# Hybrid decoder layer, input projection: all four chunks of a unit as seven half-size products, with two weight sums added by the load

## The chip, the cores and the metric

One core of a Trainium2 chip runs the whole layer. The metric is the device time of one execution in microseconds (us); the median of three runs of the kernel before is 972.0 us (971.56 to 974.65).

## What is computed

x (512 tokens by 2048, float32) is multiplied by one wide matrix; its columns feed 16 heads of 128 in three kinds (6 forgetting, 6 stick-breaking, 4 differential), each with query, key, value and gate. Each head's causal attention is multiplied by SiLU of its gate, the heads are joined, go through an output projection, and end in a layer norm:

```python
h = x @ w_in
(fq, fk, fv, fg, sq, sk, sv, sg, dq, dk, dv, dg, ff) = jnp.split(h, _split_points(), axis=-1)
...
o_fox = o_fox.reshape(b, s, FOX_W) * jax.nn.silu(fg)
...
y = jnp.concatenate([o_fox, o_sb, o_d], axis=-1) @ w_out
return _layernorm(DEEPNORM_ALPHA * x + y, ln_g, ln_b)
```

## The kernel before

Every float32 operand of a large product is cut into a high and a low part: ACT casts the high one, DVE subtracts it for the low one (`split`, L123, with `low`, L120). A product is then three matmuls, high by high, high by low and low by high (`mm3`, L111).

**Units and chunks.** Heads go in 8 pairs. A unit is one of a pair's four projections (query, key, value, gate): 256 columns of the weights by all 512 tokens, over 2048 inputs. Its weights come in four chunks of 512 inputs, 512 KB each, j = 0 to 3. The first two units are done together in eight chunks of another layout ("f"); 30 units of four chunks follow, u = 2 to 31, and then the output projection ("o"). `load_chunk` (L153) issues a chunk's load on SP's queue and its cuts on ACT and DVE, two chunks ahead of PE (`AHEAD`); raw chunks have three buffers, each cut part two.

**Seven products.** Chunks j = 1, 2, 3 (`SJ`) are taken as two-by-two blocks, with seven products of half the size in place of eight (Winograd's form of Strassen's method). `seven` (L188) makes four sums of weight blocks into the tile t (L193 two at once, L195, L196), and cuts the blocks in three tiles: a (products 1 and 2), t (5, 7, 6, 4) and d (3). The sums of the tokens' blocks are made once, by POOL, in `x_sums` (L306), out of raw tiles that `load_x` (L293) fetches while the first eight chunks run. A product is 2 k-tiles by three matmuls of 256 columns, 42 matmuls a chunk, in the order of `SEVEN`; `BANK` says which half of which PSUM bank (a to d) each goes to.

**The plain chunk.** Chunk j = 0 (`CJ`) comes last in a unit, as ordinary products straight into banks c and d: 24 products of 512 columns, of which one is taken as two halves. While it runs, ACT and DVE empty banks a and b into the tile e (L759 to L763); after it, DVE adds e to banks c and d (L786) to give the unit's two heads.

**Order of the work.** Matmuls stay in program order. `tick` (L218) counts 16 steps a unit, and `at_unit` (L215) hangs other work on a step: attention of the pairs (`attend`), and the moving of results. The other engines' order comes from the framework's planner. The second head's query and key wait in tiles of their own (`qk_tile`, L432) until `evac_later` (L436) cuts them.

## Time and profile before

| | |
|---|---|
| median of three runs | 972.0 us |
| the profiled execution | 972.67 us |
| its span, first to last instruction | 970.9 us |
| PE, DVE, ACT, POOL busy | 98%, 78%, 53%, 15% |
| bytes moved | 108.74 MB, 112 GB/s in the mean |
| granted TensorE clock, mean | 0.993 |

The span is the time between the first and the last instruction; the execution's own time adds 1.8 us. Busy shares are means over stages with different limits, so the stages are read one by one. Matmuls overlap: the time that one costs is read from one start to the next, not from its duration.

### The profile page before, as it was taken

How to read it: one execution, taken by the hardware profiler on the slowest of the kernel's cores; microseconds unless marked ns; L12 is line 12 of the kernel's file. 1: busy time of each engine (PE TensorE's matmuls, PEld its weight loads, DVE VectorE, ACT ScalarE, POOL GpSimd, SP SyncE). 2: the span in 40 equal slices, each digit the busy share in tenths (PEclk: the TensorE clock that was granted, in tenths of full speed). 3: DMA queues.
4: the chain of work that ended last, by engine and by line, in shares of the span. 5: the costliest groups of instructions: out<-in, count | busy, mean ns of one | idle time of the engine just before them, and what ended most of it. 6: DMA issues, size and time to landing. Idle time of an engine off the chain costs nothing.

```text
span 970.9 us, 16701 instructions
## 1 busy us (share of the span) xinstructions
PE 949.8 (98%) x6406; PEld 873.8 (90%) x6406; DVE 759.1 (78%) x1388; ACT 518.7 (53%) x965; POOL 141.9 (15%) x162
## 2 busy tenths in 40 slices
PE   9998999999999999999999999999999999999994
PEld 8988999999999998999899999999999988888883
DVE  7879898988898988999999888778877853442558
ACT  6556655675466556755675657446645852212222
POOL 4320211030103000110010012100201010000026
PEclk9999999999999999999999999999999999999998
DMA  7521233233223322223223333333332634833413
GB/s 282 155 79 58 99 89 122 74 109 108 98 88 98 99 87 87 85 83 105 78 90 107 109 109 99 98 99 98 109 109 98 225 100 120 325 92 104 125 38 140
DMA packets 33559, 108.74 MB, mean 112 GB/s; under 512 B 4034, under 2 KB 4674, under 8 KB 33224
## 3 DMA queue, kind: packets, MB, share of 16 engines
q1 hardware_dynamic: 29256, 95.63, 30.6%
q10 hardware_dynamic: 3744, 10.49, 3.0%
q0 software_dynamic: 480, 1.57, 0.7%
q8 instruction: 50, 0.82, 0.4%
q14 instruction: 29, 0.24, 0.1%
HBM read 99.80 MB, written 7.88 MB: 111 GB/s over the span
## 4 chain that ended last, share of the span: by engine, by line
PE 89%; DVE 5%; issue 3%; DMA 1%; ACT 1%; POOL 0%; ACTq 0%; SPq 0%; DVEq 0%; POOLq 0%
PE o L106 10%; PE l L106 3%; PE pt L109 2%; PE p0a L106 1%; PE p0b L106 1%; PE po0a L106 1%; PE po0b L106 1%; PE po0d L106 1%; PE po0c L106 1%; PE po2d L106 1%; PE po2c L106 1%; PE po2b L106 1%; PE po2a L106 1%; PE p0c L106 1%; PE p0d L106 1%
## 5 line engine op out<-in xcount | busy, mean ns | idle before, releaser
L121 DVE TENSOR_TENSOR wlt<-t,wht 128x1024 fp32r<-128x1024 f32 x90 | 110.7, 1230 | 17.9 <-ACT wht L126 17.8
L121 DVE TENSOR_TENSOR wl<-raw,wh 128x1024 fp32r<-128x1024 f32 x53 | 64.8, 1222 | 59.1 <-ACT wh L126 58.8
L126 ACT CAST wht<-t 128x1024 fp32r<-128x1024 f32 x90 | 94.3, 1048 | 28.7 <-DVE t L196 14.6
L126 ACT CAST wh<-raw 128x1024 fp32r<-128x1024 f32 x53 | 55.6, 1049 | 66.0 <-PE po2d L106 27.6
L126 ACT CAST wha<-raw 128x512 fp32r<-128x512 f32 x90 | 55.6, 619 | 48.6 <-PE p18c L106 3.6
L121 DVE TENSOR_TENSOR wla<-raw,wha 128x512 fp32r<-128x512 f32 x90 | 65.3, 727 | 15.0 <-ACT wha L126 14.7
L193 DVE TENSOR_TENSOR t<-raw 128x512 f32<-128x512 f32 x90 | 64.9, 721 | 0.5
L510 ACT ACTIVATE u<-u,m 128x128 f32<-128x128 f32 (+3 forms) x56 | 31.5, 562 | 48.8 <-DVE m L507 48.6
L121 DVE TENSOR_TENSOR wld<-raw,whd 128x256 fp32r<-128x256 f32 x90 | 50.1, 556 | 0.3
L126 ACT CAST pth<-pt 128x128 fp32r<-128x128 f32 (+1 forms) x64 | 27.0, 422 | 22.9 <-PE pt L109 22.8
L196 DVE TENSOR_TENSOR t<-raw,t 128x256 f32<-128x256 f32 x90 | 37.9, 421 | 1.5
L457 POOL TENSOR_TENSOR g<-g,ge 128x512 f32<-128x512 f32 x16 | 26.9, 1680 | 82.7 <-ACT ge L456 82.7
L195 DVE TENSOR_TENSOR t<-raw,t 128x256 f32<-128x256 f32 x90 | 38.0, 423 | 0.9
L126 ACT CAST whd<-raw 128x256 fp32r<-128x256 f32 x90 | 36.0, 400 | 4.5 <-PE p21d L106 1.6
L523 POOL TENSOR_SCALAR_AFFINE_SELECT d<-d 128x128 f32<-128x128 f32 x24 | 14.8, 618 | 158.9 <-ACT d L522 138.0
L468 POOL TENSOR_TENSOR mx<-mx,g 128x512 f32<-128x512 f32 x14 | 20.2, 1445 | 119.7 <-issue 101.1
L121 DVE TENSOR_TENSOR ptl<-pt,pth 128x128 fp32r<-128x128 f32 (+1 forms) x64 | 31.0, 484 | 5.3 <-ACT pth L126 5.0
L879 POOL TENSOR_TENSOR y<-y,gb 128x512 f32<-128x512 f32 (+1 forms) x8 | 12.0, 1517 | 157.9 <-ACT y L878 157.9
L182 DVE TENSOR_TENSOR wl<-raw,wh 128x512 fp32r<-128x512 f32 x22 | 16.0, 746 | 17.8 <-ACT wh L181 17.8
L760 DVE TENSOR_TENSOR e<-e 128x256 f32<-128x256 f32 x30 | 13.7, 456 | 18.5 <-ACT e L759 18.0
L543 POOL TENSOR_SCALAR_AFFINE_SELECT e<-e 128x128 f32<-128x128 f32 x24 | 10.4, 434 | 118.2 <-DVE e L542 90.3
L106 PE MATMUL o<-ptl,vh 128*128 128x256 f32 x96 | 26.9, 280 | 0.0
(6718 smaller groups left out, 3809.1 us busy)
## 6 DMA issues: line engine op xcount, KB each, us to landing
raw<-in_w_in_dram SPq DMA_DIRECT2D x120, 512.0 KB, 3.5
raw<-in_w_out_dram SPq DMA_DIRECT2D x32, 512.0 KB, 3.5
xr<-in_x_t_dram SPq DMA_DIRECT2D x7, 512.0 KB, 4.6
raw<-in_w_first_dram SPq DMA_DIRECT2D x7, 512.0 KB, 5.4
mixd<-mx SPq DMA_DIRECT2D x14, 256.0 KB, 2.0
mr<-mixd ACTq DMA_DIRECT2D x14, 256.0 KB, 4.1
out_dram<-y SPq DMA_DIRECT2D x14, 256.0 KB, 2.3
y<-in_x_dram ACTq DMA_DIRECT2D x4, 768.0 KB, 9.1
```

Of the source, the lines that this page charges most:

```text
L106: pin(T.matmul(ps, lhs, rhs, start=start, stop=stop))
L109: pin(T.transpose(dst, src, idt))
L121: V.tensor_tensor(out=lo, in0=src, in1=hi.bitcast(F32), op=ALU.subtract)
L126: A.copy(hi, src)
L182: pin(V.tensor_tensor(out=lo, in0=raw[:, k], in1=hi.bitcast(F32), op=ALU.subtract))
L193: V.tensor_tensor(out=t[:, 0:2], in0=raw[:, :, P:].rearrange("p (b k) c -> p b k c", b=2), in1=raw[:, 0:2].rearrange("p k (b c) -> p b k c ...
L195: V.tensor_tensor(out=t[:, 2], in0=b22, in1=t[:, 0], op=ALU.subtract)
L196: V.tensor_tensor(out=t[:, 3], in0=b21, in1=t[:, 2], op=ALU.subtract)
L457: G.tensor_tensor(out=c, in0=c, in1=e, op=ALU.mult)
L468: G.tensor_tensor(out=mx, in0=mx, in1=gt[h], op=ALU.mult)
L510: A.activation(u[:, :n], u[:, :n], AF.Exp, bias=m, scale=-1.0, accum_out=sm)
L523: G.affine_select(out=dt_[:, i * P:n], in_=dt_[:, i * P:n], pattern=[[-1, P]], base=0, channel_multiplier=1, compare_op=ALU.is_ge, fill=BIG)
```

## The change

All four chunks of a unit, in the order 0 to 3, are taken as seven products, in the order 1, 6, 5, 7, 2, 4, 3, so that both products of a bank follow each other. In the last chunk `combine` empties each bank as soon as its last product is done. The weight blocks are laid out so that all four sums are additions: SP loads the raw chunk and, apart, block b11; POOL issues a transfer of blocks 1 and 2 that adds them to the landed blocks 0 and 1; DVE makes the other two sums in place, after blocks 2 and 3 have been cut. The tokens' sums change signs to match, are made for all eight raw tiles, and take raw buffers. The tiles t, qc, kc and others go; the second head's query and key pass through a DRAM tensor `qkd`, written and read back by POOL's queue.

```diff
@@ -61,17 +61,14 @@
     return out
-SJ = (1, 2, 3)
-CJ = tuple(j for j in range(NK // 4) if j not in SJ)
 NRES = 3
 AHEAD = 2
 T0 = 32
 TU = 16
 PAIRS = [(ORDER[2 * p], ORDER[2 * p + 1]) for p in range(NK // 2)]
-SEVEN = (1, 5, 7, 6, 2, 4, 3)
+SEVEN = (1, 6, 5, 7, 2, 4, 3)
 BANK = {1: ("a", 0), 6: ("a", 1), 5: ("b", 0), 7: ("b", 1), 2: ("c", 0), 4: ("c", 1), 3: ("d", 0)}
 H2 = S // 2
-XTAGS = ["t", "ptl", "e", "pth", "ptl", "e", "ptl", "e"]
...
@@ -137,7 +134,7 @@
     NJ = NK // KC
     NU = 4 * len(PAIRS)
     chunks = [("f", 0, j) for j in range(NJ)]
-    chunks += [("u", u, j) for u in range(2, NU) for j in SJ + CJ]
+    chunks += [("u", u, j) for u in range(2, NU) for j in range(NK // 4)]
     N_OUT = len(chunks)
     chunks += [("o", g, j) for g in range(4) for j in range(NJ)]
     ready = {}
@@ -154,14 +151,9 @@
         kind, g, j = chunks[n]
         if kind == "u":
-            raw = raw_tile(f"raw{n}", [P, 4, 256])
+            raw = raw_tile(f"raw{n}", [P, 4, 2, P])
             nc.sync.dma_start(raw, w_in[g - 2, j])
-            if j in SJ:
-                ready[n] = seven(n, raw)
-            else:
-                parts = part_tiles(n, [P, 4, 256])
-                split(*parts, raw)
-                ready[n] = [tuple(t[:, k] for t in parts) for k in range(4)]
+            ready[n] = seven(n, raw, w_in[g - 2, j])
             return
         raw = raw_tile(f"raw{n}", [P, KC, 512])
         if kind == "f":
@@ -185,24 +177,23 @@
             split(*parts, raw)
             ready[n] = [tuple(t[:, k] for t in parts) for k in range(KC)]
-    def seven(n, raw):
-
-        b21, b22 = raw[:, 2:4, :P], raw[:, 2:4, P:]
-        t = wpool.tile([P, 4, 2, P], F32, tag="t", bufs=1, name=f"t{n}")
-
-        V.tensor_tensor(out=t[:, 0:2], in0=raw[:, :, P:].rearrange("p (b k) c -> p b k c", b=2),
-                        in1=raw[:, 0:2].rearrange("p k (b c) -> p b k c", b=2), op=ALU.subtract)
-        V.tensor_tensor(out=t[:, 2], in0=b22, in1=t[:, 0], op=ALU.subtract)
-        V.tensor_tensor(out=t[:, 3], in0=b21, in1=t[:, 2], op=ALU.subtract)
-        fa = part_tiles(f"a{n}", [P, 4, P], "t2")
-        split(*fa, raw[:, :, :P])
+    def seven(n, raw, src):
+
+
+        b11 = wpool.tile([P, 2, P], F32, tag="b11", bufs=2, name=f"b11_{n}")
+        nc.sync.dma_start(b11, src[:, 0])
+        nc.gpsimd.dma_start(raw[:, 0:2], src[:, 1:3], accum_op=ALU.add)
+        f1 = part_tiles(f"a{n}", [P, 2, P], "t1")
+        split(*f1, b11)
+        f2 = part_tiles(f"b{n}", [P, 2, 2, P], "t2")
+        split(*f2, raw[:, 2:4])
+
+        V.tensor_tensor(out=raw[:, 2], in0=raw[:, 2], in1=raw[:, 0], op=ALU.add)
+        V.tensor_tensor(out=raw[:, 3], in0=raw[:, 3], in1=raw[:, 2], op=ALU.add)
         ft = part_tiles(f"t{n}", [P, 4, 2, P])
-        split(*ft, t)
-        fd = part_tiles(f"d{n}", [P, 2, P], "t1")
-        split(*fd, b22)
-        return {1: [f[:, 0:2] for f in fa], 2: [f[:, 2:4] for f in fa], 3: fd,
-                5: [f[:, 0] for f in ft], 7: [f[:, 1] for f in ft],
-                6: [f[:, 2] for f in ft], 4: [f[:, 3] for f in ft]}
+        split(*ft, raw)
+        factor = {1: (f1, None), 3: (f2, 0), 2: (f2, 1), 5: (ft, 0), 7: (ft, 1), 6: (ft, 2), 4: (ft, 3)}
+        return {m: f if b is None else [s[:, b] for s in f] for m, (f, b) in factor.items()}
     def load_late(dst, src):
...
-            pool = wpool if XTAGS[n] == "t" else at
-            xraw[n] = pool.tile([P, 2, S], F32, tag=XTAGS[n], bufs=1, name=f"xr{n}")
+            xraw[n] = at.tile([P, 2, S], F32, tag=("ptl", "pth")[n % 2], bufs=1, name=f"xr{n}")
             if n > 0:
                 nc.sync.dma_start(xraw[n], xt[n])
...
-            s = wpool.tile([P, 4, H2], F32, tag="t", bufs=1, name=f"s{n}")
-            G.tensor_tensor(out=s[:, 0], in0=a21, in1=a22, op=ALU.add)
-            G.tensor_tensor(out=s[:, 1], in0=a11, in1=a21, op=ALU.subtract)
+            s = raw_tile(f"s{n}", [P, 4, H2])
+            G.tensor_tensor(out=s[:, 0], in0=a21, in1=a22, op=ALU.subtract)
+            G.tensor_tensor(out=s[:, 1], in0=a21, in1=a11, op=ALU.subtract)
             G.tensor_tensor(out=s[:, 2], in0=s[:, 0], in1=a11, op=ALU.subtract)
-            G.tensor_tensor(out=s[:, 3], in0=a12, in1=s[:, 2], op=ALU.subtract)
...
@@ -429,12 +418,18 @@
                     V.tensor_copy(tl[lr], tl[hr].bitcast(F32))
                 ks[h] = (a, b, lo)
-        def qk_tile(is_q, h):
-
-            return at.tile([P, S], F32, tag="qc" if is_q else "kc", name=f"{'q' if is_q else 'k'}c{h}")
-
         def evac_later(p, is_q, src):
-            at_unit(64 * p + SECOND[p] - (4 if is_q else 3), lambda: evac_qk(PAIRS[p][1], is_q, src))
+
+            i, u = 0 if is_q else 1, 64 * p + SECOND[p] - (4 if is_q else 3)
+            nc.gpsimd.dma_start(qkd[2 * p + i], src)
+            back = {}
+
+            def load():
+                back[0] = wk(f"{'qk'[i]}c{p}")
+                nc.gpsimd.dma_start(back[0], qkd[2 * p + i])
+
+            at_unit(u - 5, load)
+            at_unit(u, lambda: evac_qk(PAIRS[p][1], is_q, back[0]))
         def evac_v(h, s, c):
...
@@ -678,12 +673,11 @@
         load_x(2)
         split_x(1)
         for n in range(3, NJ):
-            at_unit(max(1, 4 * n - 11), lambda n=n: load_x(n))
+            at_unit(4 * n - 8, lambda n=n: load_x(n))
         for n in range(2, NJ):
             at_unit(4 * n - 6, lambda n=n: split_x(n))
         for n in range(NJ):
-            if n // 2 in SJ:
-                at_unit(4 * n + 1, lambda n=n: x_sums(n))
+            at_unit(max(1, 4 * n - 1), lambda n=n: x_sums(n))
         at_unit(40, constants)
         at_unit(24, ff_start)
...
@@ -723,81 +717,80 @@
                     if c % 2 == 0:
                         evac_qk(PAIRS[0][0], c < 2, acc[c])
                     else:
...
+                        cc = wk(f"{'q' if c < 2 else 'k'}r")
                         A.copy(cc, acc[c])
                         evac_later(0, c < 2, cc)
             del ready[n]
+        part = {}
+
+        def combine(u, pr, pb):
+
+            pair, kind = PAIRS[u // 4], u % 4
+            if pr == 6:
+
+                e = part["e"] = at.tile([P, 3, H2], F32, tag="e", name=f"e{u}")
+                A.copy(e[:, 0:3:2], pb["a"].rearrange("p (b t) -> p b t", b=2))
+                V.tensor_tensor(out=e[:, 2], in0=e[:, 0], in1=e[:, 2], op=ALU.add)
+                return
+            if pr not in (7, 4, 3):
+                return
+            e = part["e"]
+            if pr == 7:
+
+                for c in range(2):
+                    part[c] = (at.tile([P, S], F32, tag=f"g{c}", name=f"g{pair[c]}") if kind == 3
+                               else wk(f"c{u}_{c}"))
+                V.tensor_tensor(out=e[:, 1:3], in0=e[:, 2:3].to_broadcast([P, 2, H2]),
+                                in1=pb["b"].rearrange("p (b t) -> p b t", b=2), op=ALU.subtract)
+                V.tensor_tensor(out=part[1][:, H2:], in0=pb["b"][:, H2:], in1=e[:, 1], op=ALU.subtract)
+                return
+            if pr == 4:
+                c = 0
+                V.tensor_tensor(out=part[0].rearrange("p (b t) -> p b t", b=2), in0=e[:, 0:3:2],
+                                in1=pb["c"].rearrange("p (b t) -> p b t", b=2), op=ALU.add)
+            else:
+                c = 1
+                V.tensor_tensor(out=part[1][:, :H2], in0=pb["d"][:, :H2], in1=e[:, 1], op=ALU.subtract)
+            h, cc = pair[c], part[c]
+            if kind < 2 and c == 0:
+                evac_qk(h, kind == 0, cc)
+            elif kind < 2:
+                evac_later(u // 4, kind == 0, cc)
+            elif kind == 2:
+                at_unit(clock[0] + 2 + c, lambda h=h, c=c, cc=cc: evac_v(h, c, cc))
+            else:
+                at_unit(clock[0] + 2 + 3 * c, lambda h=h, cc=cc: silu(h, cc))
+
         n = NJ
         for u in range(2, NU):
...
             pb = {}
-            for pos, j in enumerate(SJ + CJ):
+            for j in range(NK // 4):
                 load_ahead(n)
                 wp = ready[n]
...
+                xp = {1: xa[j], 5: xs[j][0], 7: xs[j][1], 6: xs[j][2], 3: xs[j][3]}
+                for m, pr in enumerate(SEVEN):
+                    if m % 2 == 0:
+                        tick()
+                    b, half = BANK[pr]
+                    if b not in pb:
+                        pb[b] = bank(u, b)
+                    dst = pb[b][:, half * H2:(half + 1) * H2]
+                    for i in range(2):
+                        if pr in xp:
+                            bh, bl = xp[pr][0][:, i], xp[pr][1][:, i]
+                        else:
+                            kt, cs = 4 * j + 2 + i, slice(0, H2) if pr == 2 else slice(H2, S)
+                            bh, bl = xh[kt][:, cs], xl[kt][:, cs]
+                        mm3(dst, wp[pr][0][:, i], wp[pr][1][:, i], bh, bl,
+                            j == 0 and i == 0 and half == 0,
+                            j == NK // 4 - 1 and i == 1 and (half == 1 or pr == 3))
+                    if j == NK // 4 - 1:
+                        combine(u, pr, pb)
                 del ready[n]
                 n += 1
...
+                if u == NU - 1 and j < 2:
+                    for kt in range(7 * j, 7 * j + 7):
                         load_mix(kt)
         def out_product(n, k, kt, t, c0, ps):
...
@@ -940,7 +933,8 @@
         x_t=a["x"][0].T.reshape(NK // 4, 2, 2, P, S).transpose(0, 2, 3, 1, 4).reshape(NK // 2, P, 2, S),
         w_first=_np.concatenate([w1[..., c:c + 256] for c in units[:2]], -1).reshape(
             NK // 4, 2, 2, P, 512).transpose(0, 2, 3, 1, 4).reshape(NK // 2, P, 2, 512),
-        w_in=_np.stack([w1[..., c:c + 256].transpose(0, 2, 1, 3) for c in units[2:]]),
+        w_in=_np.stack([w1[..., c:c + 256].reshape(NK // 4, 2, 2, P, 2, P).transpose(0, 3, 1, 4, 2, 5).reshape(
+            NK // 4, P, 4, 2, P)[:, :, [0, 1, 3, 2]] for c in units[2:]]),
         w_ff=w1[..., O_FF:O_FF + NF].transpose(2, 0, 1, 3).reshape(P, NK, NF),
         w_out=w2.transpose(3, 0, 2, 1, 4),
     )
```

## Rows read from the trace of the kernel before

**Rows 1.** The page's part 1: busy us (share of the span) x instructions

```profile
PE 949.8 (98%) x6406; PEld 873.8 (90%) x6406; DVE 759.1 (78%) x1388; ACT 518.7 (53%) x965; POOL 141.9 (15%) x162
```

**Rows 2.** Waits of PE, longest first: us in total, times, longest us

```profile
PE pt L109 <- ACT rs L551: 2.7, 1, 2.7
```

**Rows 3.** Busy time by window: window, length, busy us (x) of PE, PEld, DVE, ACT, POOL, clock, DMA

```profile
100.00:340.00 240.00, 240.00 (x1771) 228.92 (x1770) 210.56 (x351) 142.46 (x258) 40.34 (x52) 1.00 0.31 99
340.00:520.00 180.00, 177.68 (x1264) 163.66 (x1264) 164.88 (x356) 111.95 (x222) 14.31 (x12) 0.99 0.27 86
520.00:740.00 220.00, 220.00 (x1641) 210.58 (x1640) 178.87 (x329) 128.07 (x237) 27.97 (x34) 1.00 0.34 105
```

**Rows 4.** Timeline of PE in unit 10: start us, us, instruction, form, count

```profile
253.53 0.28 PE L106 MATMUL p10a<-xa2h,wha 128*128 128x256 f32 x1
...
258.57 0.28 PE L106 MATMUL l<-kh,qh 128*128 128x256 f32 x1
...
264.07 0.40 PE L106 MATMUL p10c<-x0h,wh 128*128 128x512 f32 x1
...
266.82 0.33 PE L106 MATMUL l<-kh,qh 128*128 128x384 f32 x1
...
267.35 0.40 PE L106 MATMUL p10d<-x0h,wh 128*128 128x256 f32 x2
...
270.10 0.38 PE L109 MATMUL pt<-ident,rs 128*128 128x128 f32 x2
```

**Rows 5.** Matmuls by tile: count, ns least/median/most, first to last start; unit 2, then output

```profile
L106 PE MATMUL p2a<-xa1h,wha x2: 278/280/282, 50.5 to 50.8; 128*128 128x256 f32 x2
...
L106 PE MATMUL po0a<-wh,m0h x1: 388/388/388, 776.4 to 776.4; 128*128 128x512 f32 x1
```

**Rows 6.** DVE's groups: form, count | busy us, mean ns | idle before, by whom

```profile
L121 DVE TENSOR_TENSOR wlt<-t,wht 128x1024 fp32r<-128x1024 f32 x90 | 110.7, 1230 | 17.9 <-ACT wht L126 17.8
L121 DVE TENSOR_TENSOR wla<-raw,wha 128x512 fp32r<-128x512 f32 x90 | 65.3, 727 | 15.0 <-ACT wha L126 14.7
L193 DVE TENSOR_TENSOR t<-raw 128x512 f32<-128x512 f32 x90 | 64.9, 721 | 0.5
...
L121 DVE TENSOR_TENSOR wld<-raw,whd 128x256 fp32r<-128x256 f32 x90 | 50.1, 556 | 0.3
L195 DVE TENSOR_TENSOR t<-raw,t 128x256 f32<-128x256 f32 x90 | 38.0, 423 | 0.9
```

**Rows 7.** ACT's groups, the same columns

```profile
L126 ACT CAST wht<-t 128x1024 fp32r<-128x1024 f32 x90 | 94.3, 1048 | 28.7 <-DVE t L196 14.6
...
L126 ACT CAST wha<-raw 128x512 fp32r<-128x512 f32 x90 | 55.6, 619 | 48.6 <-PE p18c L106 3.6
```

**Rows 8.** Timeline, SP, DVE and PE: a usual chunk (first three), then the tightest

```profile
277.37 0.33 SPq L158 DMA_DIRECT2D raw<-in_w_in_dram  x1
...
295.31 1.22 DVE L121 TENSOR_TENSOR wlt<-t,wht 128x1024 fp32r<-128x1024 f32 x1 [0.17 <-ACT wht L126]
...
301.85 0.28 PE L106 MATMUL p12b<-xs_0h,wht 128*128 128x256 f32 x1
...
428.93 1.23 DVE L121 TENSOR_TENSOR wlt<-t,wht 128x1024 fp32r<-128x1024 f32 x1 [0.45 <-ACT wht L126]
...
430.47 0.28 PE L106 MATMUL p17b<-xs_0h,wht 128*128 128x256 f32 x1
```

**Rows 9.** Timeline, ACT and DVE: emptying banks a and b of unit 11

```profile
286.01 0.59 ACT L759 COPY e<-p11a 128x512 f32<-128x512 f32 x1 [2.37 <-PE p11a L106]
...
287.16 0.69 DVE L761 TENSOR_TENSOR e<-e,p11b 128x512 f32<-128x512 f32 x1
...
288.37 0.41 DVE L763 TENSOR_TENSOR e<-e,p11b 128x256 f32<-128x256 f32 x1
```

**Rows 10.** DMA issues: out<-in, queue, count, KB each, median us to landing

```profile
raw<-in_w_in_dram SPq DMA_DIRECT2D x120, 512.0 KB, 3.5
...
cb<-cd POOLq DMA_DIRECT2D x6, 256.0 KB, 3.6
```

More of the change, by code (lines that the diff above doesn't have):

```diff
@@ L255, in kx_pair @@
         return tuple(kx.tile(shape, F32R, tag=t, name=f"{name}{s}") for t, s in zip(tags, "hl"))
-    for j in SJ + CJ:
-        if j in SJ:
-            xa[j] = kx_pair(x_slot(j), [P, 2, H2], f"xa{j}")
-        for kt in range(4 * j + (2 if j in SJ else 0), 4 * j + 4):
+    for j in range(NK // 4):
+        xa[j] = kx_pair(x_slot(j), [P, 2, H2], f"xa{j}")
+        for kt in (4 * j + 2, 4 * j + 3):
             xh[kt], xl[kt] = kx_pair(x_slot(j), [P, S], f"x{kt}")
-        if j in SJ:
-            xs[j] = [kx_pair(x_slot(j), [P, 2, H2], f"xs{j}_{s}") for s in range(4)]
+        xs[j] = [kx_pair(x_slot(j), [P, 2, H2], f"xs{j}_{s}") for s in range(4)]
     def x_parts(kt):
@@ L276, in trunk @@
     cd = dram.tile([NF, S], F32, name="cd")
+    qkd = dram.tile([2 * len(PAIRS), P, S], F32, name="qkd")
     with ExitStack() as actx:
@@ L288, in trunk @@
         xraw = {}
-        for i, j in enumerate(SJ):
-            xb[j] = tuple(at.tile([P, 2, H2], F32R, tag=t, bufs=b, name=f"xb{j}{s}")
-                          for s, (t, b) in zip("hl", ((("g0", 1), ("g1", 1)), (("mx", 2), ("mx", 2)), (("vh0", 1), ("vl0", 1)))[i]))
+        for j in range(NK // 4):
+            tags = (("g0", "g1"), ("mx", "cb"), ("vh0", "vl0"), ("vh1", "vl1"))[j]
+            xb[j] = tuple(at.tile([P, 2, H2], F32R, tag=tag, name=f"xb{j}{s}") for s, tag in zip("hl", tags))
         def load_x(n):
-            pool = wpool if XTAGS[n] == "t" else at
-            xraw[n] = pool.tile([P, 2, S], F32, tag=XTAGS[n], bufs=1, name=f"xr{n}")
+            xraw[n] = at.tile([P, 2, S], F32, tag=("ptl", "pth")[n % 2], bufs=1, name=f"xr{n}")
             if n > 0:
@@ L310, in x_sums @@
             a11, a21, a12, a22 = r[:, 0, :H2], r[:, 0, H2:], r[:, 1, :H2], r[:, 1, H2:]
-            s = wpool.tile([P, 4, H2], F32, tag="t", bufs=1, name=f"s{n}")
-            G.tensor_tensor(out=s[:, 0], in0=a21, in1=a22, op=ALU.add)
-            G.tensor_tensor(out=s[:, 1], in0=a11, in1=a21, op=ALU.subtract)
+            s = raw_tile(f"s{n}", [P, 4, H2])
+            G.tensor_tensor(out=s[:, 0], in0=a21, in1=a22, op=ALU.subtract)
+            G.tensor_tensor(out=s[:, 1], in0=a21, in1=a11, op=ALU.subtract)
             G.tensor_tensor(out=s[:, 2], in0=s[:, 0], in1=a11, op=ALU.subtract)
-            G.tensor_tensor(out=s[:, 3], in0=a12, in1=s[:, 2], op=ALU.subtract)
+            G.tensor_tensor(out=s[:, 3], in0=a12, in1=s[:, 2], op=ALU.add)
             for m in range(4):
@@ L342, in ff_start @@
         def ff_start():
-            wf = at.tile([P, NK, NF], F32, name="wf")
+            wf = wk("wf")[:, :NK * NF].rearrange("p (a b) -> p a b", a=NK)
             load_late(wf, w_ff)
@@ L602, in head_out @@
             o = o_of[h]
-            mx = at.tile([P, S], F32, tag="mx", bufs=2, name=f"mx{h}")
+            mx = at.tile([P, S], F32, tag="mx", name=f"mx{h}")
             A.copy(mx, o)
@@ L731, in trunk @@
         n = NJ
         for u in range(2, NU):
[L733 removed]
             pb = {}
[L735 removed]
+            for j in range(NK // 4):
                 load_ahead(n)
                 wp = ready[n]
[L738 to L796 removed]
@@ L797, in trunk @@
                 del ready[n]
                 n += 1
-                if u == NU - 1 and pos < 2:
-                    for kt in range(7 * pos, 7 * pos + 7):
+                if u == NU - 1 and j < 2:
+                    for kt in range(7 * j, 7 * j + 7):
                         load_mix(kt)
```

64 lines of the change are left out of this document (3 added, 61 removed).

## Prediction

> **What bounds the kernel now.** I read the page's busy shares first: PE is busy for 949.8 us of a span of 970.9, DVE for 759.1, ACT 518.7, POOL 141.9 [rows 1]. A busy PE alone is no bound, so I read next what PE waited for. The longest wait of the whole run is 2.7 us, once [rows 2]: PE is never kept waiting for weights, and its length is the sum of its matmuls. Third, the busy time by stage: between 100 and 340 us, and between 520 and 740, PE is busy all the time, and DVE for 210.6 of 240 us and 178.9 of 220; in the differential heads' stage, 340 to 520, DVE reaches 164.9 of 180 [rows 3]. So an edit that shortens PE's stream shortens the run, as long as DVE, which stands at 81 to 92%, keeps up. Last, the timeline of PE: what is a chunk worth? In unit 10 the 42 half-size matmuls of a seven-product chunk go from 253.53 to 258.57, 5.04 us or 0.120 us each; the plain chunk's first half takes 264.07 to 266.82 and its second 267.35 to 270.10, 2.75 us each, 0.229 us per full matmul [rows 4]. The 30 units run from 50.5 to 776.4 [rows 5], 24.2 us each: 3 x 5.04 + 5.50 = 20.6 us of projection and 3.6 us of attention between.
>
> **PE, removed and added.** Each unit's plain chunk (23 full and two half matmuls) becomes a seven-product chunk like its neighbours: 5.50 becomes 5.04, 0.46 us less, and 30 units make **-13.8 us**. All of it lies on the path, since PE waits for nothing. The first eight chunks (two units together) get two more k-tiles whose tokens lie in two halves; each costs 12 products x (2 x 0.120 - 0.229) = 0.13 us, +0.3 us in all.
>
> Those are rows at the full clock. The Trainium skill, in TensorE: Matmul & The Clock Gate, section Back-to-back issue gap, gives N/2.4 + 2.5 ns between matmuls of N columns, 109 ns for 256 and 216 for 512; by that a chunk would fall from 5.18 to 4.59 us and the sum's first term would be 30 x 0.59 = -17.9 us. The trace has 120 and 229 ns [rows 4] and I keep its 13.8.
>
> **DVE and ACT.** A seven-product chunk now costs DVE a 512-wide sum (0.72), two 256-wide ones (0.42 each), and three cuts of 0.73, 1.23 and 0.56 [rows 6]: 4.08 us; a plain chunk costs one cut like the 1.23. That is 13.5 us a unit. After: cuts of 0.56, 0.73 and 1.23 and two sums of 0.42, 3.36 us, four times: 13.4. The unit's end loses a 256-wide add. So DVE does 0.3 us less per unit and has 0.46 us less time: 0.1 us per unit worse off, with 1 us to spare in the stage where it is fullest. Nothing is charged; DVE's spare time covers it. ACT gets one more 512-wide cast of 0.62 and a 256-wide one below that [rows 7], about 1 us a unit, on an engine half idle.
>
> **The load.** Beside the 512 KB of a chunk SP fetches 128 KB into a buffer of its own, and POOL issues a 256 KB transfer that adds into the landed 512 KB, so it waits for them. 120 of these. The trace has no accumulating transfer. The nearest row is POOL's own 256 KB load, 3.6 us to landing; the 512 KB weight load takes 3.5 [rows 10]. I bound the accumulate between that 3.6 and twice that, 7.2, since it must read what it adds to, and take 5. Can it hide? In the chunk shown the load is issued at 277.37 and PE uses the sums at 301.85, 24.5 us later [rows 8]; of 90 such chunks the least is 20.5. From 20.5 go 3.5 for the load, 0.6 for POOL's issue, and 3.1 for the sums, cast and cut that follow: 13 us are left for a transfer of 3.6 to 7.2. It is charged nothing; what hides it is that weights are fetched two chunks ahead, and without that cover it would cost its whole 5 us per chunk. POOL's queue behind it holds the attention masks and the gate products; they wait if the load is late, and PE's transposes after them. The second head's q and k go through DRAM and back, 32 more POOL issues with five ticks (some 7 us) of lead against two landings of 3.6; the write has nothing after it and the read has its lead, so zero.
>
> **What gets later.** Before, the three weight sums come straight from the raw chunk and are ready early; only ACT's cast (1.05) and DVE's cut (1.23) wait for PE to free their buffer, at the end of the sixth product two chunks earlier [rows 6, 7]. After, the sums are made in place over two blocks that must first be cut, and that cut's buffer is freed by the seventh product, the last. So behind PE's chunk n now stand cast 0.62, cut 0.73, sums 0.84, cast 1.05, cut 1.23: 4.5 us in a row on two engines, instead of 2.3 starting 0.72 us earlier. The slack to PE's first use falls by 0.72 + 0.62 + 0.73 + 0.84 = 2.9 us. What slack is there? The usual chunk has its cut done at 295.31 + 1.22 and used at 301.85, 5.3 us; the tightest has 428.93 + 1.23 against 430.47, 0.3 us [rows 8]. Of the 90 chunks nine have less than 2.9 us, and what they lack adds up to 11.8 us. Four of these, 7.9 us of it, stand in the differential heads' stage, where the cast had waited for a sum in a single buffer that the change removes. With them counted as cured 3.9 us are lost, uncured 11.8; I take **+5**, by the cured end, with 1 us for DVE's fullness there, which remains.
>
> **The unit's end.** The banks are now emptied while the same chunk still runs. Bank b is full after the fourth product and wanted again by the third of the next unit, 5 x 0.72 = 3.6 us later. ACT's copy and DVE's three adds, the last two of 0.69 and 0.41, took from 286.01 to 288.78 in unit 11, with one other DVE instruction slipping in between [rows 9]; only the last two need bank b, 1.1 us, and two more slipped instructions of 0.7 still fit. Before, an entire plain chunk covered this. Between 0 and 5 us; I take **+1**, as the row shown fits.
>
> **Sum.** -13.8 + 0.3 + 5 + 1 = -7.5 us. The profiled execution took 972.67 us (span 970.9 and 1.8 outside it), 0.7 above the median of 972.0 of the three runs, so 965.2 for it and **964.5** against the median.
>
> **Rivals.** (1) Slower: the weight chain. Place: DVE, between the last product of chunk n and the second of n+2. The room is one chunk and one product, 5.04 + 0.72, plus 0.9 of attention, 6.7 us; the chain needs 4.5, so it decides once other vector work delays it by over 2.2 us on average. DVE at 92% in 340 to 520 [rows 3] speaks for it, the 5 us slack of most chunks against it. If PE stands for 0.25 us in each of 120 chunks, that is +30: -13.5 + 30 = +16.5, **988 us**. (2) Much slower: the accumulate lands later than 13 us, or POOL reaches it late, and DVE stands at the sums; 1 us in each chunk is +120, some 1078 us. For it speaks only that no row prices an accumulate. The Trainium skill, SBUF — State Buffer, section Who interferes with whom, warns that a transfer issued by GpSimd can be starved of its descriptors while DVE holds the shared port; no row here shows that. (3) No change: stalls and gain cancel, DVE's stages stay as long as they are, 969 to 975. The 11.8 us of missing slack, uncured, with 2 of bank waits would do it.
>
> **Chances.** A measurement of this kernel can tell about 0.3% from no change, 969.1 to 974.9. The forecast's case, with its own range 957 to 969, has 0.53: PE's part is sure and the rest is small by most rows. No change 0.15. The weight chain 0.22, the late load 0.10. So faster 0.53, same 0.15, slower 0.32. The range goes from 957 (all of the PE gain, no stall) to 990, which takes in the weight chain's price and leaves out the late load and the worst of the chain.
>
> **What would show it.** Right: no 512-column projection matmuls in the units, unit length near 23.9, PE's waits still a few us; the chain of waits still PE's. The weight chain shows as PE waiting for the cut of the four sums (wlt), in the stage 340 to 520 first; the banks as waits of the first matmul into bank b behind DVE; the late load as DVE idle before the in-place sums, released by a DMA. The forecast is wrong if PE's waits pass 14 us in sum.

## The result and the profile after

The change makes the kernel **slower**: 1045.89 us in the median of four runs against 973.33 for the kernel before, a ratio of 1.075 (1.071 to 1.078). The profiled execution, the slowest of the four, took 1048.88 us; its span is 1047.1 us against 970.9, so 76.2 us are to be found.

These rows are from the page of the kernel after: busy shares, granted clock in 40 slices, the chain's shares by engine, landing times (the last figure of a row).

```profile
PE 967.6 (92%) x6944; PEld 910.0 (87%) x6944; DVE 758.6 (72%) x1428; ACT 552.4 (53%) x1035; POOL 258.1 (25%) x322
...
PEclk9989999999999999899989999999999999999997
...
PE 58%; DVE 20%; DMA 9%; issue 7%; ACT 5%; POOL 1%; DVEq 0%; POOLq 0%; ACTq 0%; SPq 0%
...
raw<-in_w_in_dram SPq DMA_DIRECT2D x120, 512.0 KB, 4.3
raw<-in_w_in_dram POOLq DMA_DIRECT2D x120, 256.0 KB, 4.5
```

PE was busy 98% of the span [rows 1], now 92%, and DVE's share has fallen as well: no engine is busy all the time, they wait for each other, and the chain that ended last runs over DVE for 20% of the span and over DMAs for 9%. The same stages as in [rows 3], with PE's and DVE's busy time ahead of each bracket:

```profile
100.00:340.00 240.00, 225.38 (x1817) 221.61 (x1817) 192.02 (x339) 141.70 (x262) 71.60 (x98) 0.99 0.66 162
340.00:520.00 180.00, 165.34 (x1250) 157.61 (x1251) 144.44 (x307) 103.42 (x199) 40.82 (x47) 0.95 0.62 148
520.00:740.00 220.00, 208.38 (x1648) 202.46 (x1648) 168.74 (x345) 133.50 (x251) 54.80 (x70) 0.98 0.66 167
```

In the first of these stages PE stood for 14.6 us; before, not at all. Then PE's waits, which answer to [rows 2]:

```profile
PE p2a L103 <- DVE ql L127: 7.8, 1, 7.8
PE p31a L103 <- ACT wht L123: 4.5, 1, 4.5
PE l L103 <- DVE kb L418: 4.3, 4, 1.3
PE vp L106 <- DVE c L750: 4.3, 4, 1.7
...
PE p28a L103 <- DVE wlt L118: 1.7, 1, 1.7
...
PE p9c L103 <- DVE c L750: 1.5, 1, 1.5
```

There are many places: the first unit's first bank (p2a), the four sums' cast and cut (wht, wlt), bank c at a unit's end, the transposes of v (vp), the scores (l).

**Where the 76.2 us lie.** By stage: unit 2 begins at 65.7 instead of 50.5 [rows 5], +15.2; the 30 units run to 851.4, 785.7 us instead of 725.9, +59.8; the rest +1.2. By kind, from the starts of successive matmuls: at their usual spacing (about 61, 120, 173 and 227 ns for 128, 256, 384 and 512 columns) they add up to 909.4 us (922.4 before), -13.0; gaps of over 0.15 us beyond that spacing come to 88.3 us (14.1 before), +74.2; what remains is +15. Nearly all of that is matmuls at the lower of TensorE's two clock levels: it was granted in 11 stretches, 64.3 us (14.8 before), and the matmuls there took 15.5 us over their usual spacing (1.4 before). The mean granted clock fell from 0.993 to 0.970; it is 0.87 between 60 and 100 us, around the wait of 7.8 us, and 0.95 in the stage 340 to 520.

The gaps, grouped by what the matmul behind one reads or writes, are the measure for the experiments. The three groups of the table make 49 of the 88.3 us; the rest is mainly the first products into bank a (16 us, half of it at p2a), the scores (12) and the transposes of attention (4).

| run | us | ratio | four sums (wht, wlt) | banks c, d | v's transposes | all gaps |
|---|---|---|---|---|---|---|
| before | 973.3 | 1 | 0 | 1.9 | 0 | 14.1 |
| after | 1045.9 | 1.075 (1.071 to 1.078) | 32.1 | 8.5 | 8.4 | 88.3 |
| reload by ScalarE | 1028.9 | 1.057 (1.051 to 1.063) | 24.7 | 7.6 | 9.1 | 71.7 |
| no accumulate | 1016.0 | 1.044 (1.040 to 1.048) | 19.5 | 7.9 | 8.2 | 63.4 |
| order 1 3 6 2 5 7 4 | 1069.3 | 1.099 (1.094 to 1.103) | 12.6 | 61.3 | 0.5 | 104.4 |
| x sums in work tiles | 1036.5 | 1.065 (1.061 to 1.069) | 30.2 | 8.0 | 8.7 | 80.3 |
| that order, d emptied early | 1057.6 | 1.085 (1.082 to 1.088) | 11.4 | 41.9 | 2.8 | 94.2 |
| accumulate later | 1048.1 | 1.075 (1.072 to 1.079) | 32.4 | 7.6 | 10.1 | 89.4 |
| before, accumulate added | 986.3 | 1.014 (1.008 to 1.020) | 5.8 | 1.9 | 1.0 | 22.9 |
| three sums on DVE | 1049.0 | 1.079 (1.069 to 1.089) | 23.5 | 13.3 | 17.1 | 86.2 |
| mixed order | 1042.9 | 1.072 (1.067 to 1.078) | 12.8 | 19.3 | 20.7 | 83.8 |
| sums in a tile of their own | 1052.8 | 1.083 (1.078 to 1.087) | 6.5 | 18.7 | 17.9 | 87.8 |
| no accumulate, mixed order | 1000.7 | 1.028 (1.023 to 1.033) | 6.7 | 8.5 | 12.1 | 51.3 |

**How GpSimd's queue reaches PE.** Unit 7, the timelines of POOL, ACT and DVE in turn (start, duration; in brackets the idle time and who ended it):

```profile
211.69 0.88 POOL L185 DMA_DIRECT2D raw<-in_w_in_dram  x1 [6.12 <-DMA raw<-in_w_in_dram]
212.27 0.61 POOL L538 TENSOR_SCALAR_AFFINE_SELECT e<-e 128x128 f32<-128x128 f32 x1
212.51 0.90 POOL L429 DMA_DIRECT2D kc<-qkd  x1
...
218.87 0.62 ACT L123 CAST kh<-kc 128x512 fp32r<-128x512 f32 x1 [4.75 <-DMA kc<-qkd]
...
212.91 1.23 DVE L541 TENSOR_TENSOR_SCAN rs<-e 128x512 f32<-128x512 f32 x1 [1.04 <-POOL e L538]
...
219.53 0.69 DVE L118 TENSOR_TENSOR kl<-kc,kh 128x512 fp32r<-128x512 f32 x1 [2.98 <-ACT kh L123]
220.13 0.42 DVE L192 TENSOR_TENSOR raw<-raw 128x256 f32<-128x256 f32 x1
221.66 1.23 DVE L118 TENSOR_TENSOR wlt<-raw,wht 128x1024 fp32r<-128x1024 f32 x1 [1.11 <-ACT wht L123]
```

POOL stands 6.12 us at the accumulate, because the load that it adds to has not landed. Behind it wait a mask of attention and the reload of k. The reload lands six us later; ACT has stood 4.75 us at the cast of k, DVE 2.98 at its cut, and the sum and cut of a chunk's weights behind them are late. Nothing in this row of waits is itself long work. In sum POOL stood 248.2 us in 68 places like this; DVE waited for the accumulate itself only 2.3 us, once, before the first unit.

### The profile page after: what moved, and what is told of

The parts are those of the page before. It is cut to its first block, busy times and chain, and to the rows that moved or that the text cites. A ratio compares the mean times of both kernels' runs of the same rounds, so it can differ in the third digit from the quotient of the medians.

```text
span 1047.1 us, 18681 instructions
## 1 busy us (share of the span) xinstructions
PE 967.6 (92%) x6944; PEld 910.0 (87%) x6944; DVE 758.6 (72%) x1428; ACT 552.4 (53%) x1035; POOL 258.1 (25%) x322
## 3 DMA queue, kind: packets, MB, share of 16 engines
q1 hardware_dynamic: 46536, 111.36, 34.5%
## 4 chain that ended last, share of the span: by engine, by line
PE 58%; DVE 20%; DMA 9%; issue 7%; ACT 5%; POOL 1%; DVEq 0%; POOLq 0%; ACTq 0%; SPq 0%
PE o L103 9%; DMA raw<-in_w_in_dram 4%; DMA kc<-qkd 3%; DVE wlt L118 3%; ACT wht L123 2%; PE l L103 2%; DVE wlb L118 2%; DVE wla L118 1%; DVE raw L191 1%; PE pt L106 1%; PE po0d L103 1%; PE po0c L103 1%; PE po0b L103 1%; PE po2d L103 1%; PE po2c L103 1%
## 5 line engine op out<-in xcount | busy, mean ns | idle before, releaser
L185 POOL DMA_DIRECT2D raw<-in_w_in_dram x120 | 104.7, 872 | 442.4 <-DMA raw<-in_w_in_dram 248.2
L118 DVE TENSOR_TENSOR wlt<-raw,wht 128x1024 fp32r<-128x1024 f32 x120 | 147.7, 1231 | 54.0 <-ACT wht L123 52.6
L123 ACT CAST wht<-raw 128x1024 fp32r<-128x1024 f32 x120 | 125.5, 1046 | 100.3 <-DVE raw L192 93.7
L118 DVE TENSOR_TENSOR wlb<-raw,whb 128x512 fp32r<-128x512 f32 x120 | 93.6, 780 | 37.5 <-ACT whb L123 24.4
L123 ACT CAST whb<-raw 128x512 fp32r<-128x512 f32 x120 | 74.1, 618 | 69.6 <-issue 4.8
L118 DVE TENSOR_TENSOR wl<-raw,wh 128x1024 fp32r<-128x1024 f32 x23 | 28.6, 1245 | 51.8 <-ACT wh L123 51.8
L123 ACT CAST wh<-raw 128x1024 fp32r<-128x1024 f32 x23 | 24.2, 1051 | 66.9 <-PE po2d L103 27.6
L191 DVE TENSOR_TENSOR raw<-raw 128x256 f32<-128x256 f32 x120 | 52.3, 436 | 2.6 <-DMA raw<-in_w_in_dram 2.3
L123 ACT CAST wha<-b 128x256 fp32r<-128x256 f32 x120 | 48.3, 403 | 9.5 <-PE p2a L103 1.6
L118 DVE TENSOR_TENSOR wla<-b,wha 128x256 fp32r<-128x256 f32 x120 | 51.7, 431 | 0.9 <-ACT wha L123 0.7
L192 DVE TENSOR_TENSOR raw<-raw 128x256 f32<-128x256 f32 x120 | 50.2, 419 | 1.5
L505 ACT ACTIVATE u<-u,m 128x128 f32<-128x128 f32 (+3 forms) x56 | 31.4, 561 | 20.6 <-DVE m L502 20.5
L123 ACT CAST pth<-pt 128x128 fp32r<-128x128 f32 (+1 forms) x64 | 26.9, 420 | 12.8 <-PE pt L106 12.8
L452 POOL TENSOR_TENSOR g<-g,ge 128x512 f32<-128x512 f32 x16 | 24.9, 1556 | 24.8 <-ACT ge L451 24.7
L174 DVE TENSOR_TENSOR wl<-raw,wh 128x512 fp32r<-128x512 f32 x22 | 15.9, 740 | 16.9 <-ACT wh L173 16.9
L541 DVE TENSOR_TENSOR_SCAN rs<-e 128x128 f32<-128x128 f32 (+3 forms) x24 | 22.9, 956 | 4.3 <-POOL e L538 4.3
```

The lines of the kernel that those rows point to most:

```text
L118: V.tensor_tensor(out=lo, in0=src, in1=hi.bitcast(F32), op=ALU.subtract)
L123: A.copy(hi, src)
L174: pin(V.tensor_tensor(out=lo, in0=raw[:, k], in1=hi.bitcast(F32), op=ALU.subtract))
L185: nc.gpsimd.dma_start(raw[:, 0:2], src[:, 1:3], accum_op=ALU.add)
L191: V.tensor_tensor(out=raw[:, 2], in0=raw[:, 2], in1=raw[:, 0], op=ALU.add)
L192: V.tensor_tensor(out=raw[:, 3], in0=raw[:, 3], in1=raw[:, 2], op=ALU.add)
```

## The experiments

**GpSimd's line, and the weight chain.** Two theories came first: A, the line in POOL's queue just shown; B, the chain from cut through sums to cast and cut, which fills its room by itself. First the reload alone was moved:

```diff
-                nc.gpsimd.dma_start(back[0], qkd[2 * p + i])
+                nc.scalar.dma_start(back[0], qkd[2 * p + i])
```

> Only the queue that issues the 16 reloads of the second head's q and k changes: ScalarE's instead of GpSimd's. Theory A (GpSimd stands in its queue until the 512 KB load has landed, 248 us in sum, so the reload behind it is issued late, ACT stands at the cast of q or k, 20.5 us in seven places, and the weight casts behind it are late): these ACT waits fall under 4 us and the eight last units of the pairs, together 40 us longer than before, lose 20 to 40 us; 1006 to 1026 us. Theory B (the weight chain, cut before sums before cast before cut, fills its room by itself): PE's waits for the cut of the four sums stay near 32 us, and the time stays above 1035.

1028.9 us, -17: a little less than A's least, more than B allows. POOL stood at the landing as before (242.0 us), but ACT's waits for the reload fell from 20.5 to 5.4 us (3.8 for the cast of k, 1.6 for the half-width one), and unit 7 from 29.2 to 25.5 us. But 24.7 us of gaps at the four sums stay. Both theories hold a part.

```diff
-        nc.gpsimd.dma_start(raw[:, 0:2], src[:, 1:3], accum_op=ALU.add)
```

> Leaves out the accumulating load, so two of the seven weight factors lack a summand. Theory A: GpSimd no longer stands, the masks and the reload come on time as in the run with the reload on ScalarE and the time is like that run's or up to 10 us below it, 1000 to 1020 us. Theory B: no chain of the weights had waited for the accumulate (DVE stood 2.3 us at the sums), so PE's waits for the cut stay near 32 us and the time stays above 1030. If the accumulate costs by its traffic (31 MB, 12.5% of the DMA engines' time), loads land in under 4 us instead of 4.3 and nothing else moves.

1016.0 us, -30, as A said. So the accumulate is worth 30 us in all, and the reload's route, 17 us when it alone was moved, is more than half of that. The other 13 are not separated: masks behind the accumulate, and the traffic, for a load now lands in 3.5 us instead of 4.3. The traffic is larger than the expectation has it. POOL's queue with the accumulates, then without (packets, MB, share of the DMA engines' time), differs by 19% of that time, not 12.5%:

```profile
q0 software_dynamic: 20320, 41.43, 22.1%
q0 software_dynamic: 3040, 9.96, 2.9%
```

What B holds is still there: 19.5 us.

```diff
-SEVEN = (1, 6, 5, 7, 2, 4, 3)
+SEVEN = (1, 3, 6, 2, 5, 7, 4)
```

> The same seven products in the order 1 3 6 2 5 7 4: the factors of products 3 and 2 are free after the fourth product instead of the seventh, and the sums are first needed by the third product instead of the second. Theory B: room grows by 3 x 0.72 + 0.72 = 2.9 us per chunk, PE's waits for the cast and the cut of the four sums fall from 32 us to under 8, the half clock behind them goes too, 1000 to 1015 us. Theory A alone: ACT still stands 20 us at the reloaded q and k, the last units of the pairs stay long, above 1025 us.

1069.3 us, slower. B's waits did fall, to 12.6 us, but bank d, now filled second, was emptied only at the unit's end, and PE stood at it for 61 us. The edit had made a wait of its own, so bank d got an earlier way out:

```diff
                 V.tensor_tensor(out=e[:, 2], in0=e[:, 0], in1=e[:, 2], op=ALU.add)
+                V.tensor_tensor(out=e[:, 1], in0=pb["d"][:, :H2], in1=e[:, 2], op=ALU.subtract)
...
+                V.tensor_tensor(out=part[1][:, :H2], in0=e[:, 1], in1=b5, op=ALU.add)
+                V.tensor_tensor(out=e[:, 2], in0=e[:, 2], in1=b7, op=ALU.subtract)
+                V.tensor_tensor(out=part[1][:, H2:], in0=b5, in1=e[:, 2], op=ALU.subtract)
```

> The order 1 3 6 2 5 7 4 of the run before, but bank d (product 3) is emptied into the half e1 = d - e2 right after product 6 instead of after product 7. If that run's 60 us of waits at bank d were only the late emptying, they go, and what is left shows the weight chain's price: theory B (chain of cut, sums, cast, cut too long for its room) expects PE's waits for the cast and cut of the sums to stay near 10 us instead of 32 and the time at 1005 to 1020 us. If the time is above 1035, the weight chain was only hiding another bound (DVE's and ACT's queue at the unit's end, GpSimd's line) and its 32 us come back as waits elsewhere.

1057.6 us: the second reading. The sums' gaps stay low (11.4) and come back at bank c, whose last product now closes the unit. So curing the weight chain alone buys nothing: another bound stands right behind it. Its place in the run, PE's waits:

```profile
PE p13c L103 <- DVE c L751: 4.0, 1, 4.0
PE p5c L103 <- DVE c L751: 4.0, 1, 4.0
PE p9c L103 <- DVE c L751: 4.0, 1, 4.0
```

Two more cures of the chain left the unit's end alone. One changes the order in the two middle chunks only, the other frees the sums from the cut before them:

```diff
-                for m, pr in enumerate(SEVEN):
+                for m, pr in enumerate((1, 3, 2, 6, 5, 7, 4) if j in (1, 2) else SEVEN):
```

> The changed kernel with its order of products in the first and the last chunk of a unit, and 1 3 2 6 5 7 4 in the two between: the unit's end is untouched, and the factors of products 3 and 2 come free earlier in half of the chunks. Theory B expects PE's waits for the cast and cut of the sums to fall from 32 us to about 15 and nothing to come back at the banks, 1015 to 1030 us. If the waits only move to another place again, above 1040.

```diff
+        t = wpool.tile([P, 2, 2, P], F32, tag="t", bufs=1, name=f"t{n}")
+        V.tensor_tensor(out=t[:, 0], in0=raw[:, 2], in1=raw[:, 0], op=ALU.add)
+        V.tensor_tensor(out=t[:, 1], in0=raw[:, 3], in1=t[:, 0], op=ALU.add)
...
-        split(*ft, raw)
+        split(ft[0][:, 0:2], ft[1][:, 0:2], raw[:, 0:2])
+        split(ft[0][:, 2:4], ft[1][:, 2:4], t)
```

> The changed kernel with the two sums written to a tile of their own (2 KB, work tiles six instead of seven), so they no longer wait for the cut of the blocks they add to; the cast and cut of the four factors go in two halves each (0.19 us more on ACT, 0.23 on DVE per chunk). Theory B expects the waits for the cast and cut of the sums to fall from 32 us to under 15: 1015 to 1032. If DVE's line as a whole is what is late, not this chain, the extra instructions make it no better: 1040 to 1055.

1042.9 and 1052.8 us, each in its second range: in both the sums' gaps fall (12.8 and 6.5) and the unit's end takes over, 40.0 and 36.6 us at the banks and v's transposes instead of 16.9. B as I had put it falls: the chain is one of two bounds that lie side by side. (The second of the two runs also has a work tile less, which no run tried alone.)

**The unit's end.** What makes it late? The end of unit 4 in the kernel after, DVE's timeline; product 4 ends at 151.1, bank c's sum is L750:

```profile
152.59 0.42 DVE L754 TENSOR_TENSOR c<-p4d,e 128x256 f32<-128x256 f32 x1 [0.62 <-PE p4d L103]
152.93 0.68 DVE L537 SCALAR_TENSOR_TENSOR e<-l,e 128x512 f32<-128x512 f32 x1
153.53 0.68 DVE L118 TENSOR_TENSOR wlb<-raw,whb 128x512 fp32r<-128x512 f32 x1
154.12 0.55 DVE L118 TENSOR_TENSOR ptl<-pt,pth 128x384 fp32r<-128x384 f32 x1
154.59 0.41 DVE L118 TENSOR_TENSOR wla<-b,wha 128x256 fp32r<-128x256 f32 x1
154.93 0.42 DVE L191 TENSOR_TENSOR raw<-raw 128x256 f32<-128x256 f32 x1
155.26 1.22 DVE L541 TENSOR_TENSOR_SCAN rs<-e 128x512 f32<-128x512 f32 x1
156.39 0.66 DVE L750 TENSOR_TENSOR c<-e,p4c 128x512 f32<-128x512 f32 x1
```

From 152.59 on DVE works without a pause, but bank c's sum stands behind seven other instructions. The planner put bank d's sum, attention and the next weights ahead of it. In the mixed order POOL's line joins in (unit 6, POOL and DVE):

```profile
208.85 0.86 POOL L185 DMA_DIRECT2D raw<-in_w_in_dram  x1 [5.86 <-DMA raw<-in_w_in_dram]
209.40 0.61 POOL L538 TENSOR_SCALAR_AFFINE_SELECT e<-e 128x128 f32<-128x128 f32 x1
...
210.05 0.96 DVE L541 TENSOR_TENSOR_SCAN rs<-e 128x384 f32<-128x384 f32 x1 [1.88 <-POOL e L538]
210.92 0.66 DVE L750 TENSOR_TENSOR c<-e,p6c 128x512 f32<-128x512 f32 x1
```

The scan waits for the mask, the mask stands behind the accumulate, and bank c's sum behind the scan: theory A2, a second route of the line. A run without accumulate in the mixed order was to tell it from a lack of room:

> Leaves out the accumulating load (so two of the seven weight factors lack a summand) and takes 1 3 2 6 5 7 4 in the two middle chunks of a unit. Theory A2 (GpSimd's line reaches PE also through DVE: mask behind the accumulate, DVE's scan behind the mask, the combining behind the scan): with the line gone the waits at bank c and at v's transposes, 39 us in the run with the mixed order, fall to 16 or less, those for the cut of the sums stay under 10, and the time is 990 to 1003 us. If the unit's end is short of room by itself: waits at bank c and v stay above 25 us, 1008 us or more.

1000.7 us, inside A2's range. The gaps at the banks and at v's transposes fell from 40.0 to 20.6, not to 16: the accumulate is half of them. That it acts through the mask, and not through the reload, fits a run below, in which the reload is cured and 40.1 us stay. The other half I put down to DVE's own work ahead of the sum, as in the rows of unit 4; no run isolates it. The gaps at the four sums are 6.7.

**The accumulate in the old plan.** The kernel before, its plain chunk and its combining kept, with the new way of making factors in its 90 seven-product chunks (and small constants in work tiles, to make room):

```diff
-    def seven(n, raw):
+    def seven(n, raw, src):
...
+        nc.gpsimd.dma_start(raw[:, 0:2], src[:, 1:3], accum_op=ALU.add)
...
-                        V.tensor_tensor(out=e[:, 1:4:2], in0=e[:, 2:3].to_broadcast([P, 2, H2]),
+                        V.tensor_tensor(out=e[:, 1], in0=pb["b"][:, :H2], in1=e[:, 2], op=ALU.subtract)
```

> The kernel before, with its plain fourth chunk and its combining left as they are, and only the making of the weight factors of its 90 seven-product chunks as in the change: 128 KB beside, the accumulating load, two sums in place after the cut. If the accumulating load (GpSimd's line) and the longer weight chain cause most of the loss, this alone costs three quarters of what leaving the accumulate out of the changed kernel gave back (30 us) and of its 32 us of waits for the cut: 1000 to 1020 us. If the loss comes from four sevens in a row and the earlier combining, it stays below 985.

986.3 us, 1.4% or 14.6 us more than the kernel before, under the 1000 that I expected of the accumulate, just above the other theory's 985. Its largest wait is in the first stage; in the units the cut of the sums holds PE up for less than a us at a time. POOL stands at the landing here as well:

```profile
PE p2a L106 <- DVE ql L130: 4.6, 1, 4.6
...
PE p20b L106 <- DVE wlt L121: 0.8, 1, 0.8
...
POOL raw L195 <- DMA raw<-in_w_in_dram: 114.3, 28, 11.7
```

So load, accumulate and in-place chain nearly fit into the old plan: the 30 units take 730.3 us instead of 725.9, the first stage 5.4 more. I put that down to the plain chunk, which needs no sums and no accumulate and runs while banks a and b are emptied; the fourth seven-product chunk would then have taken that cover from the weight chain and the unit's end at once. This is argued, not shown: the run also lacks the reload through DRAM, the sums of x in raw buffers, the new order of products and the early emptying of the banks.

The opposite run keeps the four sevens and takes the accumulate and the in-place sums out:

```diff
-        nc.gpsimd.dma_start(raw[:, 0:2], src[:, 1:3], accum_op=ALU.add)
+        V.tensor_tensor(out=t[:, 0:2], in0=raw[:, 0:2], in1=raw[:, 1:3], op=ALU.add)
```

> The changed kernel without the accumulating load and without the loads beside: three sums on DVE straight from the landed chunk into a tile of their own, as before the change, at 0.72 us more of DVE per chunk; work tiles six instead of seven to make room. If accumulate, GpSimd's line and the in-place chain are the loss: 990 to 1010 us in spite of 86 us more DVE work. If the room at the unit's end and DVE's line is the loss, more DVE work makes it worse: above 1040.

1049.0 us, the second reading: the line is gone, but the unit's end is worse, 30.4 us at banks and transposes. The 120 more sums keep DVE busy 825.2 us instead of 758.6, which is 66.6 more, not 86; DVE's instructions overlap a little, as in the rows of unit 4. So DVE's queue, not only what it waits for, is the likely bound there; the missing work tile is the rival that no run separates.

**The first stage.** The sums of x took raw buffers; here they take two work tiles:

```diff
-            s = raw_tile(f"s{n}", [P, 4, H2])
+            s = [t[:, k * H2:(k + 1) * H2] for t in (wk(f"sa{n}"), wk(f"sb{n}")) for k in range(2)]
```

> The sums of x's quarters go to two work tiles instead of a weight chunk's raw buffer. If the raw buffers hold up the first units' weight loads (first load of unit 2 issued at 47.6 us, the third at 56.3, and ACT stands in its queue at them with the emptying of bank a behind), the first stage loses 8 to 15 us of the 15 that it grew: 1031 to 1038 us. If DVE, full from 20 to 56 us, is what stretches it, it loses under 3 us: 1043 to 1046 us.

1036.5 us, -9.4, a time as the first theory said, and PE's wait at the first bank of unit 2 falls from 7.8 us (the row p2a above) to 0.3. But the stage itself lost only 3.9 us, not 8 or more: unit 2 begins at 61.8 instead of 65.7. The rest came later, 2.0 us in unit 2, the others spread over units on which this edit has no clear hold. What is left of the stage looks like DVE, by the windows view of the kernel after between 5 and 56 us (its busy time is the third in the row):

```profile
5.00:56.00 51.00, 46.48 (x282) 41.23 (x282) 50.95 (x76) 29.76 (x69) 29.87 (x33) 0.97 0.56 176
```

Part of its work is slow cuts. Two that follow each other, and the sum of x that POOL was making (ends at 54.40):

```profile
53.72 0.96 DVE L118 TENSOR_TENSOR xs_0l<-s,xs_0h 128x256 fp32r<-128x256 f32 x1
54.61 0.41 DVE L118 TENSOR_TENSOR xs_1l<-s,xs_1h 128x256 fp32r<-128x256 f32 x1
...
53.58 0.82 POOL L304 TENSOR_TENSOR s<-xr,s 128x256 f32<-128x256 f32 x1
```

DVE is busy for 50.95 of 51 us. That this alone explains what is left of the stage is argued from these rows and not tried by itself.

**Combinations.** They put edits shown above together, to see whether the gains add. The reload by ScalarE and the work tiles:

> The reload of q and k issued by ScalarE and the sums of x in work tiles, order of products as in the change. Separate causes: 1046 - 17 - 9 = 1020 us (1015 to 1025). The same stalls seen twice: above 1028.

1022.0 us, a ratio of 1.050 (1.044 to 1.056), in the first range: reload and first stage are separate causes. The same two with the mixed order:

> The same two edits with the mixed order of products. Under theory A2 the mask's route through DVE stays, so the waits at the unit's end stay too: 1015 to 1035, no better than without the mixed order. If the unit's end needed only the reload's route cured: 1005 or less.

1043.8 us, worse than the range: the sums' gaps fall to 13.5, the banks and transposes rise to 40.1. With the order 1 3 6 2 5 7 4 and bank d emptied early instead:

> Three edits together: the order with bank d emptied early, the reload of q and k issued by ScalarE, the sums of x in work tiles. If the weight chain, the reload behind GpSimd's line and the raw buffers of the first stage are separate causes, the gains add: 1046 - 17 - 9 - (25 to 40) = 980 to 995 us. If they are the same stalls seen twice, it stays above 1005.

1050.3 us: with this order the gains do not add. Putting the accumulate half a chunk later in the program did nothing by itself, nor with these three:

```diff
-            ready[n] = seven(n, raw, w_in[g - 2, j])
+            late[n] = lambda: ready.update({n: seven(n, raw, b11, w_in[g - 2, j])})
...
+                    if m == 4 and n + AHEAD in late:
+                        late.pop(n + AHEAD)()
```

> Only the accumulating load and the cuts behind it are put half a chunk (some 3 us) later in the program than the two loads of the same chunk. Theory A expects GpSimd to stand at the load's landing for under 130 us instead of 248 and the time to fall by 5 to 20 us, 1026 to 1041; the lost lead matters if DVE's waits for the accumulate at the sums rise from 2 us to over 15, then no gain or slower.

> The three edits and the accumulating load half a chunk later. With the masks of attention freed from GpSimd's line: 5 to 15 us under the run with the three edits, 970 to 988 us. If the masks' waits lie beside other work: within 4 us of it.

1048.1 and 1048.9 us. In the first, POOL reached the accumulate 4.8 us after the load was issued (4.9 before the edit, medians) and still stood 240.0 us at the landing: the planner had left its queue as it was. So this edit tested nothing of theory A. Last, the edits of no accumulate, mixed order and work tiles for x together:

> As the run before it, accumulating load left out, with the sums of x in work tiles. The first stage gets 4 to 10 us shorter if the raw buffers held it up, as they did with the accumulate in place (-9); nothing if the load left out had freed them already. 983 to 1000 us under theory A2.

997.3 us, in the range, but 3.4 us under the run before it, of which the first stage gave 1.1 and not 4 to 10: leaving the accumulate out had already brought unit 2's start from 65.7 to 61.2. Unit 26 takes 21.55 us, measured from its first matmul to that of unit 27, against 22.49 before (0.24 of the difference is four transposes of v that now stand in unit 27), so PE's gain is there where nothing waits. The first stage is still 9.6 us longer than before and v's transposes keep 11.5 us. No version came under the kernel before, so what the last 25 us are is in part open.

## Why the prediction was wrong

The forecast was 964.5 us, in 957 to 990; 1045.9 were measured. PE's term held. What failed is that the waits around it were priced at nearly nothing:

- **PE, -13.8 us: right.** The matmuls at their usual spacing are 13.0 us less. All of it was given back, and 73 us more.
- **The "+5" for what gets later, the weight chain: mis-sized.** It was 32 us of gaps. The chain was taken as 4.5 us of instructions in a row. For a chunk of unit 10 it began at 282.86, with the last matmul of PE's last product two chunks before (the two timelines, ACT and DVE):

```profile
283.06 0.62 ACT L123 CAST whb<-raw 128x512 fp32r<-128x512 f32 x1 [0.31 <-PE p10d L103]
286.54 1.05 ACT L123 CAST wht<-raw 128x1024 fp32r<-128x1024 f32 x1 [2.34 <-DVE raw L192]
...
283.92 0.68 DVE L118 TENSOR_TENSOR wlb<-raw,whb 128x512 fp32r<-128x512 f32 x1
284.52 0.54 DVE L118 TENSOR_TENSOR wla<-b,wha 128x256 fp32r<-128x256 f32 x1
285.23 0.42 DVE L541 TENSOR_TENSOR_SCAN rs<-e 128x128 f32<-128x128 f32 x1 [0.17 <-POOL e L538]
285.57 0.40 DVE L191 TENSOR_TENSOR raw<-raw 128x256 f32<-128x256 f32 x1
285.89 0.28 DVE L543 TENSOR_TENSOR rs<-l,rs 128x128 f32<-128x128 f32 x1
286.09 0.41 DVE L192 TENSOR_TENSOR raw<-raw 128x256 f32<-128x256 f32 x1
287.62 1.23 DVE L118 TENSOR_TENSOR wlt<-raw,wht 128x1024 fp32r<-128x1024 f32 x1 [1.12 <-ACT wht L123]
```

  The cut ends at 288.85, six us after that matmul, and PE starts the product that needs it at 289.09, here just without a wait. Three other DVE instructions stood between the links, and each hand-over costs a little. Over 118 chunks of the units the same stretch took 6.6 us in the median and 7.0 in the mean (5.0 to 14.7): 2.5 us more than 4.5, so the 2.2 us of rival 1 were reached and the room of 5.8 to 6.7 us was full. I had counted from old slack, chunk by chunk, and capped the loss at 11.8 (two of the four chunks put in the differential heads' stage lie past its end at 520). Rival 1 named this mechanism and priced it at 30. It was right on both, though not on the place, for the 32 us are 34 gaps in some 25 of the 120 chunks, 6.9 us of them in the last unit; and it still had less than half of the loss.
- **"Unit's end +1": the failed step with the widest reach.** I looked at bank b alone and let "the row shown" stand for DVE's promptness. Bank c was the one: its sum came 3.4 to 6.1 us after product 4 in the even units up to 12 (from the last matmul of the product to L750), as in the queue shown. It cost 8.5 us at the banks and 8.4 at v's transposes, where before were 1.9 and none; and each run that eased the weight chain itself, by its order or its tiles, brought more of it.
- **"It is charged nothing", the accumulate: mis-placed.** Its size was right: it landed in 4.5 us (estimate 5), and DVE waited for it once, 2.3 us. The step that failed is "they wait if the load is late": POOL waits from when its queue comes to the accumulate, whether or not the load is late for PE. Without the accumulate the time was 30 us less, its traffic included. I had named the masks as what stands behind, and then priced them by the load's lead.
- **"The write has nothing after it and the read has its lead, so zero".** The lead of five ticks was spent in POOL's queue; moving the reload alone gave 17 us back.
- **First stage, "+0.3": mis-sized**, +15.2. I priced PE's halves and not DVE's eight more cuts of sums of x, POOL's eight more adds, and the raw buffers that the sums take from the first weights, which the prediction did not mention. Giving the buffers back took 9.4 us off the whole run; DVE's share was not tried.
- **The clock was not in the sum.** About 15 us came with the gaps: ten of the eleven stretches at the lower level began while PE stood or just after it (0.95 granted in 340 to 520, 0.99 before); the eleventh is the run's end, as before.
- **The signs to look for: half right.** Waits for wlt came, as for rival 1, but the chain of waits is spread over DVE, DMA and ACT, and the sign for the late load (DVE idle before the sums, released by a DMA) stayed nearly absent though the load cost most: it worked through POOL.
